# The front of a hybrid mixer step: the conditioning constants moved to the head of the load queue, the first products and the filter steps in a new order

## The chip, the cores and the metric

The kernel runs on one core of a Trainium2 chip. Its time is the device time of one execution in microseconds (us), as the median of three runs.

Engines are TensorE (PE in the profile, its weight loads PEld), VectorE (DVE), ScalarE (ACT), GpSimd (POOL) and SyncE (SP, which issues most loads). Each engine works through its own queue of instructions in order and waits on semaphores of the others.

## The reference

One layer of a hybrid mixer for 128 prompt tokens and 512 sample tokens, D = 1024. Everything begins with an adaptive modulation and one wide projection:

```python
def modulation(cond, w_ada, b_ada):
    mod = jax.nn.silu(cond) @ w_ada + b_ada
    return jnp.split(mod, 3, axis=-1)
...
    shift, scale, gate = modulation(cond, p["w_ada"], p["b_ada"])
    h = x * (1 + scale) + shift
    (v_h, x1, x0, g_h), (q, k, v, g_a), m = split_projection(h, p["w_in"], p["conv_w"], p["conv_b"])
```

There are two conditions, one for the prompt and one for the samples. From h one branch computes a gated long convolution (Hyena), whose filters come from a small network with two sine layers:

```python
    hf = jnp.sin(f_freq[0] * (z @ f_w1 + f_b1))
    hf = jnp.sin(f_freq[1] * (hf @ f_w2 + f_b2))
    hf = (hf @ f_w3).astype(jnp.float32).reshape(L, 2, D_HYENA)
```

The other branch is a neighbourhood attention. Both are gated, projected, merged, projected again, and a layer norm closes the step.

## The kernel before

**Numbers.** Products are made in three passes of a faster fp32 type: operands are split into a high and a low part (`hH`, `hL` of h, `wf`, `wg` of a weight in the front, `wh`, `wl` behind it), and hH·wf, hH·wg and hL·wf are summed. One such pass over one block of 128 rows is two matmuls, one for each half of the 640 tokens; one product of a row in the front is thus six matmuls.

**The front** is `prologue()`. It walks over the eight blocks k of 128 channels ("rows" here). For each row

- SP loads two tiles of `wada` (ada k and ada 8+k, 512 KB each, the shift and the scale), and one tile `xw` (the block of x, and of the weights of three output tiles 0, 8 and 1; 512 KB),
- TensorE multiplies the condition `st` with them (`adaT`, 16 matmuls, which the trace shows as 32 records since these run as full fp32 in two steps), ScalarE copies the result to `row` (L315), TensorE turns it to columns (`modT`, L342), and DVE adds the bias (`mod`, L347),
- ScalarE makes hH (L355), DVE makes hx (L354), wg (L357) and hL (L358),
- TensorE adds the row's products to three pairs of banks ("0k", "8k", "1k").

The script sets where the products stand: `script[k]` has four places, ahead of ada k, ahead of ada 8+k, ahead of modT and behind hL. In row k stand the products of row k-1, so that TensorE has work while mod is made. An item "w17" is 17 filler matmuls on zeros.

**The condition.** `st` is the silu of the condition, made of `pack0` (L297 to L300: tanh on ScalarE, two steps on DVE). pack0 (17 KB) is loaded by ScalarE's queue. All other loads here go through SP in the order of the program; a load also waits where its buffer is not free yet.

**The filter network** runs beside it as a generator of small steps (`sin_layer`, L225 to L246): matmuls `ps_f` and their release from PSUM by DVE, five to six steps of range reduction on DVE, and the sine on ScalarE. `layers[k]` says how many steps are taken in row k behind the row copy, and how many behind the products. Its input `zemb` is padded to 128 rows. The PSUM banks for adaT, modT and ps_f rotate over one pool of four buffers, of which the third pair of banks (`mm1lo`, `mm1hi`) holds two.

Behind the front, a list scheduler orders the Hyena stage by its own rules; its decisions depend on what came before. There ScalarE splits weights (`wl` L159, `wh` L161; GpSimd's accumulating load L160 completes wl), copies finished projections (`zs`), applies the short convolution (`x`, `u` L556, with `tap` L559 that GpSimd adds at L560), and splits filter tiles (`sh`, L111), which TensorE transforms in `fa` (L168).

Of the kernel before, what the change touches and what calls it, by code (L numbers as in the profile page):

```python
# [49 lines left out]
def tile_hyena_natten_step(ctx: ExitStack, tc: tile.TileContext, a, o):  # L50
# [14 lines left out]

    def load_to(dst, src, eng=None):
        ins = (eng or nc.sync).dma_start(dst, src)
        last[:] = [ins]
        if pinned[0]:
            tc.keep_in_program_order(ins)  # L70
# [50 lines left out]

    def load_pack(i, eng=None):
        pack = const.tile([P, sum(n for _, n in PACKS[i])], F32, tag=f"pack{i}", name=f"pack{i}")
        load_to(pack[:], a[f"pack{i}"], eng)
        c0 = 0
        for name, n in PACKS[i]:
            out[name] = pack[:, c0 : c0 + n]
            c0 += n

    v_d = dram.tile([4, P, 1280], F32, tag="v_d", name="v_d")  # L130

    load_pack(0, nc.scalar)
    cc, sel = out["cc"], out["sel"]
# [41 lines left out]
    def accumulate(ps, w, k, xh, xl, lead=(0, 1, 2)):  # L175
        passes = (w[0], xh), (w[0], xl), (w[1], xh)
        for i in lead:
            wt, x = passes[i]
            for hf in range(2):
                nc.tensor.matmul(  # L180
                    ps[hf][:, :HALF], wt[k], x[:, hf * HALF : (hf + 1) * HALF],
                    start=(i == 0 and k == 0), stop=(i == lead[2] and k == NK - 1), skip_group_check=True,
                )
# [41 lines left out]
    def sin_layer(fs, products, dst):  # L225
# [3 lines left out]
        for i, r0, w, x in products:  # L229
            at = {} if len(ps) == 1 else dict(tile_position=(64 * i, r0))  # L230
            nc.tensor.matmul(ps[i][r0 : r0 + w.shape[1], :320], w, x, start=True, stop=True, skip_group_check=True, **at)
        for i, p in enumerate(ps):
            nc.vector.tensor_scalar(ar[:, 320 * i : 320 * i + 320], p[:, :320], fs[:, 0:1], fs[:, 1:2], op0=ALU.add, op1=ALU.mult)
# [36 lines left out]
    def prologue():  # L270
        script = (
            ("w17", "", "w2", "w6"), ("", "", "00", "80 10"), ("", "", "01", "81 11"), ("", "", "02", "82 12"),
            ("", "", "03", "83 13"), ("", "", "04", "84 14"), ("", "", "05", "85 15"), ("", "", "06", "86 16 07 87 17"),
        )
        layers = ((0, 0), (0, 2), (0, 3), (0, 3), (1, 1), (0, 2), (0, 2), (0, 1))
        nc.vector.memset(f(hid[:, :256]), 0.0)
# [3 lines left out]
        def work(items):  # L280
            for item in items.split():
# [3 lines left out]
                else:  # L285
                    i, j = int(item[0]), int(item[1])
                    c = P * front.index(i)
                    accumulate(banks[i], [{j: t[:, c : c + P]} for t in parts[j]], j, hH[:, j], hL[:, j], lead=(0, 2, 1))

# [16 lines left out]
        for k in range(NK):  # L306
            xw = wp.tile([P, 1024], F32, tag="raw", bufs=3, name=f"xw{k}")
            psa = aux(f"adaT{k}")
            pool, tag = ((hw, "X"), (hyc, "dftL"), (hw, "F"))[k % 3]
            wt = pool.tile([P, 2048], F32, tag=tag, name=f"ada{k}")  # L310
            for part in range(2):
                work(script[k][part])
                ada(part * 8 + k, psa[:, part * P : part * P + P], wt[:, 1024 * part : 1024 * part + 1024])
            row_ = hwa.tile([P, 2 * P], F32, tag="fb", bufs=3, name=f"row{k}")
            nc.scalar.activation(row_[:], psa[:, : 2 * P], AF.Copy)  # L315
            load_to(xw[:], a["xw"][k])
            if k == 1:
                out["zemb"] = temp("u", "zemb", 4)[:, :448]
                load_to(out["zemb"], a["zemb"])
                load_pack(1)  # L320
# [18 lines left out]
            psm = aux(f"modT{k}")  # L339
            work(script[k][2])  # L340
            for c in range(2):
                nc.tensor.matmul(  # L342
                    psm[:, c * 2 : c * 2 + 2], row_[:, c * P : c * P + P], sel,
                    start=True, stop=True, skip_group_check=True,
                )
            mod = const.tile([P, 2, 2], F32, tag="mod", bufs=4, name=f"mod{k}")
            nc.vector.tensor_tensor(  # L347
# [4 lines left out]
            for c, s0, n in ((0, PC, LP), (1, SC, LS)):  # L352
                cs = slice(s0, s0 + n)
                nc.vector.tensor_scalar(hx[:, cs], xt[:, cs], mod[:, 1, c : c + 1], mod[:, 0, c : c + 1], op0=ALU.mult, op1=ALU.add)  # L354
                nc.scalar.activation(hH[:, k, cs], xt[:, cs], AF.Identity, scale=mod[:, 1, c : c + 1], bias=mod[:, 0, c : c + 1])  # L355
            if k < 6:
                nc.vector.tensor_tensor(wl, wf, f(wh), op=ALU.subtract)  # L357
# [7 lines left out]
            work(script[k][3])  # L365
            step(layers[k][1])
        now(filt)
# [1262 lines left out]
def _host_constants():  # L1630
    f32 = np.float32
    zs, decs = [], []
    for L in (LS, LP):
# [10 lines left out]
        else:  # L1644
            zs.append(z)
            decs.append(dec)
    zemb = np.zeros((128, 320))
    for i, z in enumerate(np.split(np.concatenate(zs, 0), 2)):
        zemb[64 * i : 64 * i + 33] = z.T
    decay = np.stack(decs).reshape(5, 128, 4, 256).transpose(1, 2, 0, 3)  # L1650
# [36 lines left out]
def _layout(inp):  # L1687
# [11 lines left out]
    b_ada = g["b_ada"][0]  # L1699
    fw1 = np.zeros((128, 128), np.float32)  # L1700
    for i in range(2):
        fw1[64 * i : 64 * i + 33, 64 * i : 64 * i + 64] = g["filt_w1"][0]
    w3 = g["filt_w3"][0].reshape(64, 2, 4, 256).transpose(0, 2, 1, 3).reshape(64, 4, 512)
# [70 lines left out]
```

## Time and profile before

| | us |
|---|---|
| median of 3 runs (860.24 to 860.34) | 860.33 |
| the profiled execution | 860.97 |
| its span | 859.1 |
| TensorE busy in the span | 846.8 |
| VectorE busy | 690.4 |
| ScalarE busy | 479.6 |
| GpSimd busy | 174.2 |

The span is the time from the first to the last instruction of the profiled execution; the rest of its 860.97 us lies around it. Busy time is an average over the whole; where TensorE stands idle and what ended that idle time is read from the waits and the timeline. "Releaser" is the instruction or transfer whose end let a waiting one start.

### The profile page before, as it was taken

The page shows a single profiled execution, that of the slowest core. Times are in us where ns is not written, and L with a number is a line of the kernel's source. Part 1 is how long each engine was busy: PE and PEld are TensorE (multiplying, and loading weights), DVE is VectorE, ACT ScalarE, POOL GpSimd, SP SyncE. Part 2 cuts the span into 40 slices and gives each one's busy share as a digit, 9 for nine tenths or more (in the row PEclk, how much of TensorE's full clock was granted, in tenths as well). Part 3 has the DMA queues.
Part 4 walks back from the last instruction along what each step waited for, and adds up shares of the span by engine and source line. Part 5 has one row for each costly group of instructions (what it writes and reads, how often), then busy time and mean ns, then how long its engine had stood idle before and what let it go on. Part 6 is the DMA issues. An engine that isn't in the chain of part 4 may idle for free.

```text
span 859.1 us, 16879 instructions
## 1 busy us (share of the span) xinstructions
PE 846.8 (99%) x6363; PEld 820.2 (95%) x6363; DVE 690.4 (80%) x1408; ACT 479.6 (56%) x1032; POOL 174.2 (20%) x172
## 2 busy tenths in 40 slices
PE   8999999999999999999999999999999999999996
PEld 7899999999999999999999999999999999999885
DVE  4786698697597688799797998989888678799776
ACT  4485666666656446566565565656656554345310
POOL 0010250242244010132222322224222200000000
PEclk9999999999999999999999999999999999999998
DMA  9896566566555677742636353454363386445621
GB/s 359 323 273 146 113 139 133 134 140 132 130 139 114 169 176 200 249 147 70 207 121 218 88 183 126 114 172 154 96 178 114 119 264 215 159 126 150 247 100 49
DMA packets 58120, 139.28 MB, mean 162 GB/s; under 512 B 8628, under 2 KB 25144, under 8 KB 58040
## 3 DMA queue, kind: packets, MB, share of 16 engines
q1 hardware_dynamic: 45944, 113.09, 39.7%
q0 software_dynamic: 5184, 18.09, 12.9%
q10 hardware_dynamic: 6912, 7.03, 2.4%
q8 instruction: 50, 0.82, 0.4%
q14 instruction: 30, 0.25, 0.1%
HBM read 120.76 MB, written 17.43 MB: 161 GB/s over the span
## 4 chain that ended last, share of the span: by engine, by line
PE 94%; DVE 2%; DMA 2%; POOL 1%; ACT 1%; issue 0%; DVEq 0%; SPq 0%
PE sp L1222 35%; PE mm L180 27%; PE out L1591 6%; PE v L950 5%; PE pt L1060 3%; PE s L1067 3%; PE s L1020 2%; DMA ada<-wada 2%; PE mm L194 2%; PE ve L962 1%; DVE wb L112 1%; POOL x L560 1%; PE yb L168 1%; PE yb L169 1%; PE yb L170 1%; PE ut L621 1%
## 5 line engine op out<-in xcount | busy, mean ns | idle before, releaser
L1222 PE MATMUL sp<-t,wb 128*128 128x320 f32 x1008 | 157.7, 310 | 0.1
L1222 PEld LDWEIGHTS sp<-t,wb 128*128 128x128 f32 x1008 | 149.1, 188 | 1.8 <-DVE wb L112 0.6
L1222 PE MATMUL sp<-hH,wb 128*128 128x320 f32 x504 | 121.6, 312 | 0.0
L111 ACT ACTIVATE wb<-s 128x512 fp32r<-128x512 f32 x100 | 61.1, 628 | 56.8 <-DVE s L1182 31.8
L180 PE MATMUL mm<-hL,wh 128*128 128x320 f32 x384 | 92.1, 309 | 0.0
L180 PE MATMUL mm<-hH,wh 128*128 128x320 f32 x384 | 91.5, 310 | 0.0
L180 PE MATMUL mm<-hH,wl 128*128 128x320 f32 x384 | 91.5, 309 | 0.0
L1222 PEld LDWEIGHTS sp<-hH,wb 128*128 128x128 f32 x504 | 86.5, 188 | 2.0 <-issue 1.8
L160 POOL DMA_DIRECT2D wl<-wall x33 | 28.7, 870 | 242.2 <-ACT wl L159 187.3
L1222 PE MATMUL sp<-hL,wb 128*128 128x320 f32 x252 | 77.7, 308 | 0.0
L112 DVE TENSOR_TENSOR wb<-s,wb 128x512 fp32r<-128x512 f32 x100 | 67.4, 686 | 4.4 <-ACT wb L111 4.3
L1042 POOL TENSOR_SCALAR p<-p,sm 128x384 f32<-128x384 f32 x32 | 46.9, 1476 | 108.8 <-DVE sm L1041 108.8
L111 ACT ACTIVATE wb<-raw 128x512 fp32r<-128x512 f32 x72 | 45.2, 628 | 42.5 <-PE sp L1222 30.6
L180 PEld LDWEIGHTS mm<-hL,wh 128*128 128x128 f32 x384 | 65.4, 188 | 0.6
L180 PEld LDWEIGHTS mm<-hH,wh 128*128 128x128 f32 x384 | 65.2, 188 | 0.6
L180 PEld LDWEIGHTS mm<-hH,wl 128*128 128x128 f32 x384 | 65.0, 188 | 0.1
L112 DVE TENSOR_TENSOR wb<-raw,wb 128x512 fp32r<-128x512 f32 x72 | 50.5, 702 | 5.0 <-ACT wb L111 5.0
L180 PE MATMUL mm<-yhs,wh 128*128 128x320 f32 x256 | 47.9, 309 | 0.0
L1222 PEld LDWEIGHTS sp<-hL,wb 128*128 128x128 f32 x252 | 47.3, 188 | 0.0
L161 ACT ACTIVATE wh<-raw 128x1024 fp32r<-128x1024 f32 x33 | 34.9, 1057 | 22.2 <-PE mm L180 14.0
L1237 DVE TENSOR_TENSOR c<-sp,u 128x320 f32<-128x320 f32 x75 | 36.2, 483 | 13.6 <-PE sp L1222 13.6
L1042 POOL TENSOR_SCALAR edge<-edge,sm 128x320 f32<-128x320 f32 x32 | 41.6, 1309 | 0.7 <-DVE sm L1041 0.5
(397 smaller groups left out, 2137.4 us busy)
## 6 DMA issues: line engine op xcount, KB each, us to landing
raw<-wall SPq DMA_DIRECT2D x93, 512.0 KB, 3.6
wl<-wall POOLq DMA_DIRECT2D x33, 512.0 KB, 5.8
ada<-wada SPq DMA_DIRECT2D x16, 512.0 KB, 9.5
tm<-bias SPq DMA_DIRECT2D x16, 512.0 KB, 4.7
xw<-xw SPq DMA_DIRECT2D x8, 512.0 KB, 8.4
gate<-wgate SPq DMA_DIRECT2D x8, 512.0 KB, 3.7
wo<-wall SPq DMA_DIRECT2D x8, 512.0 KB, 5.7
dec<-decay SPq DMA_DIRECT2D x20, 128.0 KB, 4.3
```

The costliest lines, as they stand in the source:

```text
L111: hi = nc.scalar.activation(dst_h, src, AF.Copy)
L112: return hi, (eng or nc.vector).tensor_tensor(dst_l, src, f(dst_h), op=ALU.subtract)
L160: nc.gpsimd.dma_start(wl, a["wall"][i], accum_op=ALU.add)
L161: nc.scalar.activation(wh, raw[:], AF.Copy)
L180: nc.tensor.matmul(ps[hf][:, :HALF], wt[k], x[:, hf * HALF : (hf + 1) * HALF], start=(i == 0 and k == 0), stop=(i == lead[2] and k == NK - ...
L950: nc.tensor.matmul(ps[t // 2][:, t % 2 * 256 : t % 2 * 256 + 256], x[:, k, P * t : P * t + P], wk, start=first and t % 2 == 0, stop=last, ...
L1042: nc.gpsimd.tensor_scalar_mul(pv, pv, sm[:, 2:3])
L1060: nc.tensor.transpose(pt[:, i * P : i * P + P], x, ident)
L1067: nc.tensor.matmul(dst, lhs, rhs, start=start, stop=stop, skip_group_check=True)
L1222: nc.tensor.matmul(dst, wk, x(xi, k), start=j < 4 and k == 0 and i == 0, stop=k == 3 and i == 2, skip_group_check=True,)
L1237: after = nc.vector.tensor_tensor(c, dst, c if j == 3 else u, op=ALU.add)
L1591: ins = nc.tensor.matmul(dst, m[k][:, c0 : c0 + P], w[:, c : c + n], start=(first and k == 0), stop=(last and k == 5), skip_group_check=True,)
```

## The change

1. pack0 is loaded by SP, first of all; the argument for another queue goes.
2. In row 0, 19 fillers instead of 17 stand ahead; one filler (before: two) now between the two modT matmuls; six behind as before. The row copy is made in two halves, each behind its half of adaT. DVE makes hH of the prompt columns, and wg ahead of hx.
3. Row 0's products are cut: "00a" are the passes with hH of product 0, "00b" the one with hL. In rows 1 and 2 they stand in other places, and row 2's two ada halves have product "01" between them.
4. `layers` has three numbers: the second counts steps behind modT. The first sine layer yields once more, behind its matmuls. In effect the first sine stands in row 4 instead of at the end of row 3, and the matmuls of the second layer behind modT of row 4.
5. zemb and its weights `fw1` are packed into 66 rows (2 x 33) instead of 128.

```diff
-    load_pack(0, nc.scalar)
+    load_pack(0)
...
+        yield
         for i, p in enumerate(ps):
             nc.vector.tensor_scalar(ar[:, 320 * i : 320 * i + 320], p[:, :320], fs[:, 0:1], fs[:, 1:2], op0=ALU.add, op1=ALU.mult)
         yield
...
         script = (
-            ("w17", "", "w2", "w6"), ("", "", "00", "80 10"), ("", "", "01", "81 11"), ("", "", "02", "82 12"),
+            ("w19", "", "w1", "w6"), ("00a", "", "80a", "10a 00b 80b 10b"), ("", "01", "81", "11"), ("", "", "02", "82 12"),
             ("", "", "03", "83 13"), ("", "", "04", "84 14"), ("", "", "05", "85 15"), ("", "", "06", "86 16 07 87 17"),
         )
-        layers = ((0, 0), (0, 2), (0, 3), (0, 3), (1, 1), (0, 2), (0, 2), (0, 1))
+        layers = ((0, 0, 0), (0, 0, 3), (0, 0, 3), (0, 0, 2), (1, 1, 2), (0, 0, 2), (0, 0, 2), (0, 0, 2))
+        passes = {"": (0, 2, 1), "a": (0, 2), "b": (1,)}
...
-                    accumulate(banks[i], [{j: t[:, c : c + P]} for t in parts[j]], j, hH[:, j], hL[:, j], lead=(0, 2, 1))
+                    accumulate(banks[i], [{j: t[:, c : c + P]} for t in parts[j]], j, hH[:, j], hL[:, j], lead=passes[item[2:]])
...
-            row_ = hwa.tile([P, 2 * P], F32, tag="fb", bufs=3, name=f"row{k}")
-            nc.scalar.activation(row_[:], psa[:, : 2 * P], AF.Copy)
+                if k == 0 or part:
+                    cs = slice(P * part if k == 0 else 0, P * part + P)
+                    nc.scalar.activation(row_[:, cs], psa[:, cs], AF.Copy)
...
-                out["zemb"] = temp("u", "zemb", 4)[:, :448]
+                out["zemb"] = temp("u", "zemb", 4)[:66, :448]
...
-            work(script[k][2])
+            if k:
+                work(script[k][2])
             for c in range(2):
+                if k == 0 and c:
+                    work(script[k][2])
...
+            step(layers[k][1])
...
-                nc.vector.tensor_scalar(hx[:, cs], xt[:, cs], mod[:, 1, c : c + 1], mod[:, 0, c : c + 1], op0=ALU.mult, op1=ALU.add)
-                nc.scalar.activation(hH[:, k, cs], xt[:, cs], AF.Identity, scale=mod[:, 1, c : c + 1], bias=mod[:, 0, c : c + 1])
-            if k < 6:
+                high = hH[:, k, cs], xt[:, cs]
+                scale, bias = mod[:, 1, c : c + 1], mod[:, 0, c : c + 1]
+                if k == 0 and c == 0:
+                    nc.vector.tensor_scalar(*high, scale, bias, op0=ALU.mult, op1=ALU.add)
+                    nc.vector.tensor_tensor(wl, wf, f(wh), op=ALU.subtract)
+                else:
+                    nc.scalar.activation(*high, AF.Identity, scale=scale, bias=bias)
+                nc.vector.tensor_scalar(hx[:, cs], xt[:, cs], scale, bias, op0=ALU.mult, op1=ALU.add)
+            if 0 < k < 6:
                 nc.vector.tensor_tensor(wl, wf, f(wh), op=ALU.subtract)
...
-            step(layers[k][1])
+            step(layers[k][2])
...
-    zemb = np.zeros((128, 320))
-    for i, z in enumerate(np.split(np.concatenate(zs, 0), 2)):
-        zemb[64 * i : 64 * i + 33] = z.T
+    zemb = np.concatenate([z.T for z in np.split(np.concatenate(zs, 0), 2)], axis=0)
...
-    fw1 = np.zeros((128, 128), np.float32)
+    fw1 = np.zeros((66, 128), np.float32)
     for i in range(2):
-        fw1[64 * i : 64 * i + 33, 64 * i : 64 * i + 64] = g["filt_w1"][0]
+        fw1[33 * i : 33 * i + 33, 64 * i : 64 * i + 64] = g["filt_w1"][0]
```

TensorE's queue from the start up to the second row's modT. "mm_0" and "mm_1" are the halves of product 0, hid holds the zeros of the fillers, and the number behind a name tells one buffer from another. Before:

```order
1 L284 MATMUL mm_0_131<-hid 128x256 x17
2 L265 MATMUL adaT_138<-ada_139,st 32x128 x16
3 L284 MATMUL mm_0_131<-hid 128x256 x2
4 L342 MATMUL modT_181<-pack_85,row_175 128x2 x2
5 L284 MATMUL mm_0_131<-hid 128x256 x6
6 L265 MATMUL adaT_202<-ada_203,st 32x128 x16
7 L180 MATMUL mm_0_131<-hH,wf_178 128x320
```

After:

```order
1 L286 MATMUL mm_0_131<-hid 128x256 x19
2 L266 MATMUL adaT_138<-ada_140,st 32x128 x16
3 L349 MATMUL modT_184<-pack_85,row_139 128x2
4 L286 MATMUL mm_0_131<-hid 128x256
5 L349 MATMUL modT_184<-pack_85,row_139 128x2
6 L286 MATMUL mm_0_131<-hid 128x256 x6
7 L180 MATMUL mm_0_131<-hH,wf_181 128x320
8 L180 MATMUL mm_1_132<-hH,wf_181 128x320
9 L180 MATMUL mm_0_131<-hH,wg_182 128x320
10 L180 MATMUL mm_1_132<-hH,wg_182 128x320
11 L266 MATMUL adaT_204<-ada_206,st 32x128 x16
```

Four products of row 0 have moved from behind the second adaT to ahead of it.

TensorE's queue in row 4, at the second sine layer's matmuls. hf is the first sine's result. Before:

```order
67 L265 MATMUL adaT_388<-ada_389,st 32x128 x16
68 L231 MATMUL ps_f_413<-hf_262,pack_227 128x320
69 L231 MATMUL ps_f_414<-hf_262,pack_227 128x320
70 L180 MATMUL mm_0_131<-hH,wf_351 128x320
```

After, from the last of product 0:

```order
75 L180 MATMUL mm_1_132<-hL,wf_353 128x320
76 L349 MATMUL modT_416<-pack_85,row_390 128x2 x2
77 L231 MATMUL ps_f_425<-hf_264,pack_233 128x320
78 L231 MATMUL ps_f_426<-hf_264,pack_233 128x320
```

The two matmuls have moved past six products and past modT.

ScalarE's queue where the Hyena stage begins (L556 is the short convolution, L570 in the new line numbers; L159 and L161 make the parts of the weight tile behind the next projection). Before:

```order
57 L553 ACTIVATE zs_107<-mm_1_132 128x8x40
58 L159 ACTIVATE wl_1036<-raw_1033 128x1024
59 L556 ACTIVATE u_669<-zs_107,pack_599 128x641
60 L382 ACTIVATE dftH<-draw 128x640 x2
61 L556 ACTIVATE u_723<-zs_115,pack_599 128x641
62 L161 ACTIVATE wh_1035<-raw_1033 128x1024
```

After:

```order
55 L567 ACTIVATE zs_107<-mm_1_132 128x8x40
56 L570 ACTIVATE u_671<-zs_107,pack_601 128x641
57 L396 ACTIVATE dftH<-draw 128x640 x2
58 L570 ACTIVATE u_725<-zs_115,pack_601 128x641
59 L159 ACTIVATE wl_1038<-raw_1035 128x1024
60 L161 ACTIVATE wh_1037<-raw_1035 128x1024
```

The first part of wl has moved behind four other activations. Further on the split `sh` of a filter tile has moved past three taps and part of a short convolution. Before:

```order
134 L556 ACTIVATE x_1_1473<-zs_107,pack_599 128x128
135 L559 ACTIVATE tap_17_0_1585<-zs_107,pack_599 128x128
136 L556 ACTIVATE x_1_1473<-zs_107,pack_599 128x512
137 L559 ACTIVATE tap_17_0_1588<-zs_107,pack_599 128x128
138 L559 ACTIVATE tap_17_129_1592<-zs_107,pack_599 128x512
139 L111 ACTIVATE sh_0_1152<-sd_1_1148 128x512
```

After:

```order
132 L570 ACTIVATE x_1_1475<-zs_107,pack_601 128x128
133 L111 ACTIVATE sh_0_1154<-sd_1_1150 128x512
134 L573 ACTIVATE tap_17_0_1587<-zs_107,pack_601 128x128
135 L570 ACTIVATE x_1_1475<-zs_107,pack_601 128x512
136 L573 ACTIVATE tap_17_0_1590<-zs_107,pack_601 128x128
```

Only one short convolution is left ahead of it.

## Rows read from the trace of the kernel before

**Rows 1.** Page, part 4: the chain that ended last, share by engine.

```profile
PE 94%; DVE 2%; DMA 2%; POOL 1%; ACT 1%; issue 0%; DVEq 0%; SPq 0%
```

**Rows 2.** Busy by stretch: length, busy time of each engine, clock, DMA share, GB/s.

```profile
0.00:45.00 45.00, 41.43 (x458) 36.51 (x459) 27.10 (x61) 21.46 (x40) 0.87 (x16) 1.00 0.90 340
...
20.00:25.00 5.00, 5.00 (x86) 4.55 (x78) 4.16 (x10) 2.00 (x4) 0.00 (x0) 1.00 1.03 415
```

**Rows 3.** TensorE's waits from 0 to 46 us: total, times, longest.

```profile
PE adaT L265 <- DMA ada<-wada: 0.9, 1, 0.9
PE ps_f L231 <- ACT hf L244: 0.7, 1, 0.7
PE adaT L265 <- DVE st L300: 0.5, 1, 0.5
```

**Rows 4.** Timeline, row 0: start, busy us, engine, line, instruction, [idle before <-releaser].

```profile
4.89 0.22 ACT L297 ACTIVATE th<-pack 128x16 f32<-128x16 f32 x1 [2.45 <-DMA pack<-pack]
...
5.66 1.69 PE L265 MATMUL adaT<-ada,st 128*32 128x128 f32 x32 [0.49 <-DVE st L300]
...
8.70 1.20 ACT L355 ACTIVATE hH<-xw,mod 128x128 fp32r<-128x128 f32 x2 [0.48 <-DVE mod L347]
```

**Rows 5.** DMA issues, 0 to 40 us: count, size, median us from issue to landing.

```profile
pack<-pack ACTq DMA_DIRECT2D x1, 17.0 KB, 4.1
```

**Rows 6.** Chain of the first 48 us, pieces in order: start, us, what.

```profile
0.73 0.39 SPq L67
...
6.03 9.92 DMA ada<-wada
```

**Rows 7.** Timeline of TensorE, row 2's second half, then all of row 3.

```profile
15.99 0.65 PE L265 MATMUL adaT<-ada,st 128*32 128x128 f32 x16 [0.95 <-DMA ada<-wada]
...
19.84 1.08 PE L265 MATMUL adaT<-ada,st 128*32 128x128 f32 x32
20.85 0.56 PE L180 MATMUL mm<-hH,wf 128*128 128x320 f32 x2
...
21.82 0.50 PE L342 MATMUL modT<-pack,row 128*128 128x2 f32 x4
22.19 0.54 PE L180 MATMUL mm<-hH,wf 128*128 128x320 f32 x2
...
24.13 1.08 PE L265 MATMUL adaT<-ada,st 128*32 128x128 f32 x32
```

**Rows 8.** Timeline of all engines around the second sine layer, row 4.

```profile
23.80 0.83 DVE L358 TENSOR_TENSOR hL<-hx,hH 128x640 fp32r<-128x640 f32 x1
...
25.80 0.37 ACT L315 ACTIVATE row<-adaT 128x256 f32<-128x256 f32 x1
25.94 1.07 PE L231 MATMUL ps_f<-hf,pack 64*128 64x320 f32 x4 [0.74 <-ACT hf L244]
...
26.79 1.13 DVE L233 TENSOR_SCALAR E<-ps_f,pack 128x320 f32<-128x320 f32 x2 [1.40 <-PE ps_f L231]
...
30.23 0.97 PE L265 MATMUL adaT<-ada,st 128*32 128x128 f32 x28
```

**Rows 9.** Timeline and landings around the weight tile wl10.

```profile
50.72 1.06 ACT L159 ACTIVATE wl<-raw 128x1024 fp32r<-128x1024 f32 x1 [0.26 <-DMA raw<-wall]
51.68 0.91 ACT L556 ACTIVATE u<-zs,pack 128x641 f32<-128x641 f32 x1
52.49 1.35 ACT L382 ACTIVATE dftH<-draw 128x640 fp32r<-128x640 f32 x2
...
52.11 1.00 POOL L160 DMA_DIRECT2D wl<-wall  x1 [50.70 <-ACT wl L159]
...
60.65 0.31 PE L180 MATMUL mm<-hH,wl 128*128 128x320 f32 x1
...
DMA to landing us min/median/max: 5.2/5.8/8.5
```

**Rows 10.** Timeline of TensorE where the front's Hyena filter is transformed.

```profile
118.08 0.39 PE L168 MATMUL fa<-sh,dftH 128*128 128x256 f32 x1 [0.63 <-ACT sh L111]
```

More of the change, by code (lines that the diff above doesn't have):

```diff
@@ L64, in tile_hyena_natten_step, with load_to @@
     last = []
-    def load_to(dst, src, eng=None):
-        ins = (eng or nc.sync).dma_start(dst, src)
+    def load_to(dst, src):
+        ins = nc.sync.dma_start(dst, src)
         last[:] = [ins]
@@ L120, in tile_hyena_natten_step, with load_pack @@
     yu_d, yh_d, ya_d, mh_d, ma_d = (dram.tile([NK, P, NT], F32, tag=t, name=t) for t in ("yu_d", "yh_d", "ya_d", "mh_d", "ma_d"))
-    def load_pack(i, eng=None):
+    def load_pack(i):
         pack = const.tile([P, sum(n for _, n in PACKS[i])], F32, tag=f"pack{i}", name=f"pack{i}")
-        load_to(pack[:], a[f"pack{i}"], eng)
+        load_to(pack[:], a[f"pack{i}"])
         c0 = 0
@@ L181, in accumulate @@
                     ps[hf][:, :HALF], wt[k], x[:, hf * HALF : (hf + 1) * HALF],
-                    start=(i == 0 and k == 0), stop=(i == lead[2] and k == NK - 1), skip_group_check=True,
+                    start=(i == 0 and k == 0), stop=(i == lead[-1] and k == NK - 1), skip_group_check=True,
                 )
@@ L308, in prologue @@
             psa = aux(f"adaT{k}")
+            row_ = hwa.tile([P, 2 * P], F32, tag="fb", bufs=3, name=f"row{k}")
             pool, tag = ((hw, "X"), (hyc, "dftL"), (hw, "F"))[k % 3]
```

## The prediction

> **What bounds the kernel now.** I read the chain of work that ended last first, then the busy times of the stretch that the change touches, then TensorE's waits in it, and last the timeline around each wait. The chain is 94% TensorE [rows 1], so time is won only where TensorE stands idle or does less. In the first 45 us, which hold all eight rows of the front, it is busy 41.43 us [rows 2]: 3.57 us are idle. Three waits in it have a name that the change touches: 0.5 us for the condition `st`, 0.9 us for a wada tile, 0.7 us for the filter network's first sine [rows 3]. They sum to 2.1 us. Behind the front one more wait matters: 0.63 us at 118.08 us, where `fa` waits for ScalarE's `sh` [rows 10].
>
> One more resource is full in the front: the load queue. At 20 to 25 us it moves 415 GB/s at a DMA share above 1 [rows 2]. A 512 KB tile then takes 524,288 B / 415 GB/s = 1.26 us, and a row's three tiles take 3.8 us. A row that waits for nothing takes TensorE 24.13 - 19.84 = 4.29 us [rows 7]. So TensorE is the slower of the two, but the stream starts behind it: only the first rows can be bound by data.
>
> All sums are made against the profiled execution, 860.97 us, of which 859.1 are the span. It lies 0.64 us above the median of 860.33 us; I take gains from the trace and subtract them from the median.
>
> **Part 1, the condition first.** `pack0` was issued on ScalarE's queue and took 4.1 us to land [rows 5]; the tanh waited for it until 4.89 us, and TensorE 0.49 us for `st` [rows 4]. At the head of SP's queue it should need no more than those 4.1 us, and with nothing beside it less: I take 2 to 2.5 us, an estimate from the 4.1 us that it took beside five 512 KB loads, with 4.1 as the other end. Then `st` is there well before the fillers end. The price is on SP: every load behind it is issued one issue later, 0.39 us by the chain's first piece [rows 6]. Against this, zemb shrinks from 128 to 66 rows of 1,792 B: 111 KB less, 0.27 us at 415 GB/s. So the stream behind row 1 moves by +0.39 - 0.27 = +0.12 us; bounds: -0.27 (pack0 costs the stream nothing) and +0.39 (the short zemb saves nothing).
>
> No row here has a tile of 66 partitions. A rule speaks against the saving: the Trainium skill, "DMA: Bandwidth & Descriptors", section "Why a DMA increments its semaphore by 16 and not by 1", says that such a transfer runs on the largest number of engines up to 16 that divides the row count, for 66 rows 11 engines. By it eleven engines carry six rows each instead of eight, and a later tile that needs all sixteen would gain only a quarter of zemb's old 0.55 us, 0.14 us. The stream would then move by +0.25 us, within the bounds above.
>
> **Part 2, rows 0 to 2.** Two more fillers stand in the 0.49 us of waiting, and adaT0 starts somewhere between 5.17, where the old fillers end, and the old 5.66 us [rows 4]; I take 5.4. A wait is added: the second half of adaT0 writes the bank from which ScalarE copies the first half, so it waits for that copy, at most the 0.37 us of a whole row copy [rows 8] plus the releases. Everything on TensorE is queued behind it. With the second copy, mod0 is no earlier than before, 0 to 0.3 us later. But the first products no longer need hL0, only hH0, of which ScalarE now makes one piece (before: 1.20 us for two, from 8.70 us, [rows 4]): ready at about 9.55 us.
>
> From there TensorE has work without a break. I take the spacings of an undisturbed row [rows 7]: adaT 1.01, six products 0.97, modT 0.37, twelve products 1.94 (0.16 each); the two zemb matmuls are half of four `ps_f` at 1.07 [rows 8], 0.5. Four products (9.55 to 10.2), adaT1 (11.2), four products (11.85), modT1 (12.2), ten products (13.8), zemb (14.3), first half of adaT2 (14.8), row 1's first six products (15.8). The second half of adaT2 needs the tile that came at 6.03 + 9.92 = 15.95 [rows 6]: with the stream's +0.12 it starts at 16.1 instead of 15.99. So the 0.95 us of waiting [rows 7] become about 0.3, and six products that lay behind that wait lie ahead of it. Then half an adaT (0.5), six products, modT2, six products: adaT3 can start at 18.9 instead of 19.84. Now data is late: two tiles follow the one of 15.95 before ada11, which lands at 15.95 + 3 x 1.26 = 19.73, plus 0.12. The second half of adaT3 starts at 19.9, and the row's products at 20.4 instead of 20.85. **Gain about 0.4 us**; at the bounds of the stream 0.15 and 0.85. If mod0 is 0.3 us late, this data wait swallows it.
>
> Row 3's tiles are 3.8 us further on and TensorE's next row 4.29 us: from row 4 the data is ahead.
>
> **Part 3, the filter steps.** In row 4 the four `ps_f` matmuls stood right behind adaT4 and waited 0.74 us for the sine `hf`, until 25.94 us [rows 8]. Now they stand behind six products and modT4, 0.97 + 0.37 us later on the queue: at about 26.1 us with the 0.4 us gained. The sine follows DVE's work of row 3 and one more row copy on ScalarE and should be there by 25.8. The wait goes: **0.74 us**. What is late next? DVE now takes `ps_f` out of its banks behind hL4, not ahead of mod4, and adaT5 needs one of these banks. hL3 ended at 24.63, 2.81 us behind the start of modT3 [rows 7, 8]. With modT4 at 25.6, hL4 ends at 28.4, the first half of the two additions (1.13 us, [rows 8]) at 29.0, the second at 29.5. adaT5 is ready at 30.23 - 1.14 = 29.1 [rows 8]. The first bank is in time, the second would cost 0.4 us: I take 0, since the banks come free in turn, and keep 0.4.
>
> The front thus ends about 1.14 us earlier (0.9 to 1.6).
>
> **Part 4, behind the front.** The edits also change the scheduler's order through the Hyena stage. Two places matter. At 118 us `sh` ran on ScalarE behind a tap that waits for GpSimd. In the new order sh stands ahead of all but one of the row's short-convolution steps and of all its taps. So the 0.63 us go [rows 10], unless another wait takes their place: **0.63 us**, the other end 0.
>
> The other place gets worse: wl10. ScalarE's part of it now stands behind two `u` activations and two `dftH` copies instead of ahead of them. By their spacing, 0.81 us for a u and 1.26 for the copies (about their 1.35 of busy time less the overlap, [rows 9]), it starts 2.88 us after 50.46 (where the old one still waited 0.26 us for data), at 53.34 on the old clock. GpSimd's accumulating load is issued 1.39 us behind (50.72 to 52.11), at 54.73, and lands 5.8 us later at the median: 60.53. TensorE needs it at 60.65 [rows 9]. The slack is 0.12 us instead of 2.7. The landings of these loads go from 5.2 over 5.8 to 8.5 us; nearest is the median, which costs nothing, but the slack is less than their scatter. I charge 0.2 us and keep 0 and 2.6.
>
> **The sum.** 0.4 + 0.74 + 0.63 - 0.2 = 1.57 us; 860.33 - 1.57 = **858.8 us**.
>
> **Rivals.**
> - *Data-bound*: the stream loses the whole 0.39 us, and the split's wait pushes row 0. Then rows 0 to 3 give 0.15 us instead of 0.4, the rest stays: 859.0. For: a DMA share above 1. Against: zemb is shorter.
> - *The waits move*: the sine's wait returns as adaT5's wait for its bank (0.4), and the fa wait is replaced by one of like size in the Hyena stage, where ScalarE, DVE and GpSimd release each other by turns: 0.4 + 0.74 - 0.4 - 0.2 = 0.54, so 859.8. For: a view of waits shows no slack, and the order of many rows changes. Against: before, only one such wait reached TensorE there.
> - *Slower*: wl10's load lands like the slowest of its kind, 8.5 us after issue [rows 9]. Then TensorE stands 2.6 us at about 59.5 us; with 1.14 us gained in the front and the fa wait unchanged the end is 860.33 + 1.44 = 861.8. It costs something from a landing above 5.9 us and makes the change slower from 7.1 us. Against: the median of the 33 loads is 5.8 us.
> - *It doesn't do what it says*: pack0 lands 4.1 us after issue at the head of SP's queue as well, `st` stays at 5.4 us, the split's wait comes on top, and only the filter wait is won: 859.6.
>
> **How the numbers follow.** Forecast 0.50 (858.3 to 859.2), waits that move 0.28, data-bound 0.12, slower 0.05, not as it says 0.05. The range goes from the upper ends of the front and of fa (1.6 + 0.63, less a little for wl10: 858.2) to the second rival with the low end of the front (0.9 - 0.4 - 0.2 = 0.3: 860.0). A measurement of this kernel tells about 0.2% from no change, 1.7 us. Faster than 858.6 is the better part of the forecast, 0.33; slower than 862.05 is the slow rival with a lost front besides, 0.03; the rest, 0.64, is within.
>
> **What would show it.** Right: the tanh near 3 us instead of 4.89 and no wait for `st`; the wait for ada at row 3's second half and a short one in row 2; no wait of `ps_f` for hf, and adaT5 1.1 us earlier than 30.23; no wait of fa at 117 us. Wrong: a wait of adaT5 for DVE, one of mm for wl at 59 to 60 us, or waits between 45 and 840 us that sum to more than 0.7 us. The forecast fails most easily in the Hyena stage, where slack is not visible.

## The result and the profile after

The changed kernel took 862.04 us (median of 16 runs, 861.69 to 862.59) where the kernel before took 860.34 in the same runs (859.80 to 860.69): +1.70 us, a ratio of 1.0020 with an interval of 1.0012 to 1.0027. The forecast was 858.8, in a range of 858.2 to 860.0.

In the front the waits went as the prediction said. TensorE's waits from 0 to 46 us and from 46 to 840 us in the changed kernel (total, times, longest), against [rows 3] and [rows 10]:

```profile
PE mm L286 <- DVE hid L278: 1.2, 1, 1.2
PE adaT L266 <- ACT row L319: 0.4, 1, 0.4
PE mm L180 <- DVE wg L366: 0.3, 1, 0.3
...
PE mm L180 <- DMA wl<-wall: 1.2, 1, 1.2
PE fb L169 <- DVE sl L112: 0.7, 1, 0.7
PE fb L168 <- ACT sh L111: 0.6, 1, 0.6
```

The three waits of the front that the change aimed at are gone, and so is the one of `fa`. In their place stand the predicted wait for the row copy (0.4) and one of 0.3 us for `wg`, and behind the front three new ones that sum to 2.5 us. The timeline of the changed kernel, against [rows 4] and [rows 8]:

```profile
2.62 0.21 ACT L299 ACTIVATE th<-pack 128x16 f32<-128x16 f32 x1 [0.62 <-DMA pack<-pack]
...
5.53 0.64 PE L266 MATMUL adaT<-ada,st 128*32 128x128 f32 x16
6.57 0.64 PE L266 MATMUL adaT<-ada,st 128*32 128x128 f32 x16 [0.40 <-ACT row L319]
...
25.78 1.13 PE L231 MATMUL ps_f<-hf,pack 64*128 64x320 f32 x4
...
28.79 1.08 PE L266 MATMUL adaT<-ada,st 128*32 128x128 f32 x32
```

The tanh runs at 2.62 instead of 4.89 us, `ps_f` waits for nothing, and adaT5 starts 1.44 us before the 30.23 of [rows 8].

That 1.44 us is too much, because the profiled execution of the kernel before was late. Two more profiles of the unchanged kernel (below) took 860.53 and 860.34 us, with adaT5 at 29.99 and 29.68 us. The one at 860.34, exactly the median, is the better base. Its busy times by stretch (length, busy time of PE first, ...), and then those of the changed kernel:

```profile
0.00:45.00 45.00, 41.52 (x462) 36.67 (x463) 27.65 (x63) 22.04 (x43) 0.87 (x16) 1.00 0.91 344
45.00:117.00 72.00, 71.89 (x498) 71.11 (x497) 51.85 (x78) 47.71 (x99) 16.11 (x14) 1.00 0.67 163
117.00:119.00 2.00, 1.47 (x9) 1.38 (x10) 1.49 (x2) 2.00 (x6) 1.30 (x1) 1.00 0.06 12
119.00:840.00 721.00, 720.90 (x5330) 701.13 (x5329) 596.03 (x1245) 407.59 (x886) 156.27 (x141) 1.00 0.54 154
```

```profile
0.00:45.00 45.00, 43.02 (x469) 37.80 (x470) 28.77 (x64) 22.87 (x46) 0.87 (x16) 1.00 0.92 348
45.00:117.00 72.00, 70.76 (x490) 69.91 (x490) 54.91 (x80) 46.89 (x95) 16.74 (x14) 1.00 0.64 160
117.00:119.00 2.00, 2.00 (x16) 2.00 (x15) 1.90 (x2) 1.38 (x2) 1.16 (x2) 1.00 0.03 8
119.00:840.00 721.00, 719.58 (x5321) 699.63 (x5320) 591.95 (x1240) 408.00 (x890) 154.88 (x142) 1.00 0.53 154
```

TensorE's idle time goes from 0.11 to 1.24 us in the second stretch, from 0.53 to 0 in the third, from 0.10 to 1.42 in the fourth: +1.92 us. The front gives 29.68 - 28.79 = 0.89 back. The balance is +1.03 us of the 1.4 by which the spans differ (858.5 and 859.9). (The profiled execution of the changed kernel, 861.69 us, is the fastest of its 16, so the spans show 1.4 of the 1.70 us between the medians.)

The last 0.4 us lie at the same waits. Matmuls of 0.31 us start 0.15 us apart, so their records overlap, and the idle time of a wait is counted only from the end of the last record. The changed kernel around the wait for wl:

```profile
59.35 0.31 PE L180 MATMUL mm<-hL,wh 128*128 128x320 f32 x1
60.91 0.56 PE L180 MATMUL mm<-hH,wl 128*128 128x320 f32 x2 [1.24 <-DMA wl<-wall]
61.31 0.45 PE L180 MATMUL mm<-hH,wh 128*128 128x320 f32 x2
```

Without the wait the pair behind it would have started at 59.50 us. It started 1.41 us later, and its first record was longer, so that the next pair followed 0.40 us behind and not 0.29: 1.52 us are lost, not 1.24. The waits at `fb` and the old one at `fa` cost 0.26 to 0.27 us beside their idle time in the same way (their first matmuls took 0.39 instead of 0.28 us). Three such waits came and one went, 0.54 us by this estimate. From adaT5 to the first `v` matmul at 273 us the changed kernel takes 2.37 us more (244.30 against 241.94), where idle time alone gives 2.56 - 0.63 = 1.93 and the estimate 2.47.

### The profile page after: what moved, and what is told of

Same layout as the page of the kernel before. It is cut to its first block, busy times and chain, and to the rows that moved or that the text cites. A ratio compares the mean times of both kernels' runs of the same rounds, so it can differ in the third digit from the quotient of the medians.

```text
span 859.9 us, 16885 instructions
## 1 busy us (share of the span) xinstructions
PE 847.3 (99%) x6364; PEld 820.0 (95%) x6364; DVE 691.5 (80%) x1409; ACT 479.7 (56%) x1032; POOL 173.7 (20%) x172
## 4 chain that ended last, share of the span: by engine, by line
PE 91%; DMA 3%; ACT 2%; DVE 2%; POOL 1%; issue 0%; SPq 0%; DVEq 0%
PE sp L1236 35%; PE mm L180 25%; PE out L1605 6%; PE v L964 5%; PE pt L1074 3%; PE s L1081 3%; PE s L1034 2%; DMA ada<-wada 2%; PE mm L194 2%; PE ve L976 1%; DMA wl<-wall 1%; POOL x L574 1%; DVE wb L112 1%; PE yb L169 1%; PE yb L168 1%; PE yb L170 1%
## 5 line engine op out<-in xcount | busy, mean ns | idle before, releaser
L161 ACT ACTIVATE wh<-raw 128x1024 fp32r<-128x1024 f32 x33 | 34.9, 1059 | 32.7 <-PE mm L180 24.5
```

The lines of the kernel that those rows point to most:

```text
L161: nc.scalar.activation(wh, raw[:], AF.Copy)
```

## The experiments

All were compared with the kernel before on the same chip. Ratios are to those runs.

| kernel | us, median (runs) | ratio, 95% interval |
|---|---|---|
| e1: the change, old filter steps | 860.37 (11) | 0.9998, 0.9990 to 1.0007 |
| e2: before, new filter steps alone | 862.60 (5) | 1.0033, 1.0020 to 1.0046 |
| e3: the change, old loads | 862.45 (6) | 1.0030, 1.0018 to 1.0041 |
| e4: before, new loads alone | 860.17 (11) | 0.9995, 0.9986 to 1.0004 |
| e5, e8: before, unchanged | 860.53, 860.34 (1 each) | |
| e6: the change, wl10 ahead | 859.46 (11) | 0.9990, 0.9981 to 0.9999 |
| e7: the change, one step moved | 860.00 (11) | 0.9995, 0.9986 to 1.0004 |
| e9: the change, wl3 without its load | 860.15 (11) | 0.9998, 0.9989 to 1.0006 |
| e10, e12: old rows, wl10 ahead | 859.17, 859.30 (11 each) | 0.9988, 0.9979 to 0.9997; 0.9987, 0.9978 to 0.9996 |
| e11: as e10, wh10 later | 858.80 (11) | 0.9978, 0.9970 to 0.9987 |

**Which part brings the loss?** The filter steps were undone alone, and done alone; the order of the scheduler's instructions told beforehand that the Hyena stage turns from the old order into the new one with this part, and with no other.

```diff
# e1, against the change
-        layers = ((0, 0, 0), (0, 0, 3), (0, 0, 3), (0, 0, 2), (1, 1, 2), (0, 0, 2), (0, 0, 2), (0, 0, 2))
+        layers = ((0, 0, 0), (0, 0, 2), (0, 0, 3), (0, 0, 3), (1, 0, 1), (0, 0, 2), (0, 0, 2), (0, 0, 1))
...
-        yield
         for i, p in enumerate(ps):
```

> The changed kernel with the filter network's steps where they stood before (the first sine at the end of row 3, the second layer's matmuls right behind adaT4, no extra yield). With it the Hyena stage has the order of the kernel before again, but for a few rows at its start. Theory A (the new order of the Hyena stage, which the filter steps bring about, costs more than the front wins): the front keeps the gain of rows 0 to 3, 0.8 us by the trace (row 3's products at 20.07 instead of 20.85), loses the 0.74 us of the sine's wait again, and has no wait for wl at 61 us nor for fb at 122 and 124 us: about 859.5 us, 0.8 below the kernel before. Theory B (the first products without low parts, the split row or the loads cost time that shows in the medians): the time stays above 861.

```diff
# e2, against the kernel before
-        layers = ((0, 0), (0, 2), (0, 3), (0, 3), (1, 1), (0, 2), (0, 2), (0, 1))
+        layers = ((0, 0, 0), (0, 0, 3), (0, 0, 3), (0, 0, 2), (1, 1, 2), (0, 0, 2), (0, 0, 2), (0, 0, 2))
...
+            step(layers[k][1])
             mod = const.tile([P, 2, 2], F32, tag="mod", bufs=4, name=f"mod{k}")
...
-            step(layers[k][1])
+            step(layers[k][2])
...
+        yield
         for i, p in enumerate(ps):
```

> The kernel before with the new filter steps alone. The Hyena stage then has the order of the changed kernel. Theory A: the front wins 0.74 us at ps_f and nothing else, the wl wait (1.2 us) and the two fb waits (1.3 us) appear and the fa wait (0.6 us) goes: 860.3 - 0.74 + 1.9 = about 861.5 us. Theory B: 859.6 us (only the filter wait goes).

e1 came back to 860.37 us and has neither the wl wait nor one for fb: the loss is the new order of the Hyena stage. But it did not reach 859.5, so the 0.8 us that I had read as the gain of rows 0 to 3 are not there. e2 has the three new waits in its trace (1.3, 0.7 and 0.6 us), and is 1.1 us slower than expected even so. About half of that is what two waits more cost beside their idle time (0.54 us, see above); the rest stays open. Its profiled execution shows something else, in the timeline and in the view by stretch:

```profile
5.32 0.22 ACT L298 ACTIVATE th<-pack 128x16 f32<-128x16 f32 x1 [2.88 <-DMA pack<-pack]
...
6.08 1.93 PE L266 MATMUL adaT<-ada,st 128*32 128x128 f32 x32 [0.92 <-DVE st L301]
...
10.95 1.94 PE L266 MATMUL adaT<-ada,st 128*32 128x128 f32 x32
...
17.14 1.08 PE L266 MATMUL adaT<-ada,st 128*32 128x128 f32 x32
```

```profile
6.00:8.00 2.00, 1.92 (x33) 1.42 (x33) 0.17 (x3) 1.04 (x2) 0.00 (x0) 1.00 1.03 420
```

In this execution (864.43 us, the upper end of e2's five; the lower three lie at 862.3 to 862.6) pack0, on ScalarE's queue, came at 5.3 us, TensorE waited 0.92 us, and then the 32 records of adaT took 1.93 and 1.94 us in rows 0 and 1, and 1.08 from row 2 on. The granted clock of 1.00 in the view by stretch says nothing for that time: the trace's first clock record, of the full clock (2.4 GHz), begins at 13.94 us, and the view counts time without a record as 1.00. Ahead of the first record matmuls are longer in every profile that has some on both sides of it: a filler takes 0.42 us ahead and 0.28 behind at the median, and a record of adaT in e2 and e3 0.42 and 0.27. That record begins at 4.7 to 7.4 us in twelve of the fourteen profiles, and at 13.94 and 14.08 us in those of e2 and e3 (864.77 us, the upper end of e3's six). There adaT5 starts at 31.17 and 31.53 us, against 28.62 to 28.93 in the other profiles with the new filter steps. So these two executions lost over 2 us to a slow start; why TensorE stayed slow for so long in them stays open.

**The loads.**

```diff
# e3, against the change (e4 is the reverse, against the kernel before)
-    load_pack(0)
+    load_pack(0, nc.scalar)
...
-                out["zemb"] = temp("u", "zemb", 4)[:66, :448]
+                out["zemb"] = temp("u", "zemb", 4)[:, :448]
```

> The changed kernel with pack0 on ScalarE's queue again and zemb padded to 128 rows again. Theory A: the Hyena order stays the changed one. st comes at 5.4 us, as before, so adaT0 starts near 5.7 and its second half, which waits for the first row copy, ends near 7.7 instead of 7.2; row 1 and 2 are 0.5 us later unless the second half of adaT2 or row 3 waits for data anyway: 0 to 0.5 us above the changed kernel, 862.0 to 862.5 us. Theory B: if pack0 at the head of the load queue is what costs, the time falls to about 861 or below.

> The kernel before with pack0 first on SP's queue and the short zemb alone. The Hyena order is that of before. Theory A: the 0.49 us for st go, but row 1's second half waited for its tile until 10.0 us anyway and row 2's until 15.95, so the sum moves only with the stream: 860.3 us, within 0.3 either way. Theory B: the stream is later by one issue and the time rises by 0.4 us or more.

e3 is at the upper end of what theory A expected, e4 within its bounds. In e4 adaT5 starts at 29.54 us, and row 2 waits for no tile (row 1 for one, 0.56 us). So the new loads do no harm, and are worth 0.14 to 0.45 us in the front against the two later profiles of the kernel before. By intervals the time of e4 cannot be told from no change.

**Was the base disturbed?** e5 and e8 are the unchanged kernel.

> The kernel before, unchanged, profiled once more. Its first profiled execution took 0.6 us more than its median. Theory A (the 0.95 us wait for ada10 in row 2 belonged to that one execution): the wait is shorter by some 0.5 to 0.7 us, adaT5 starts at 29.5 to 29.8 us instead of 30.23, and the span is near 858.4. Theory B (the wait belongs to the kernel): adaT5 at 30.2 us, and what rows 0 to 3 won was lost elsewhere.

> The kernel before, profiled a third time, as a second look beside the other one: the same expectations. If the two differ in row 0 or 2, what differs is the scatter that pack0's landing or one tile's landing brings.

The second half of adaT2 in e5, then in e8, against 15.99 in [rows 7]:

```profile
15.74 0.64 PE L265 MATMUL adaT<-ada,st 128*32 128x128 f32 x16 [1.10 <-DMA ada<-wada]
```

```profile
15.44 0.64 PE L265 MATMUL adaT<-ada,st 128*32 128x128 f32 x16 [0.80 <-DMA ada<-wada]
```

Neither theory is quite right: the wait belongs to the kernel (0.80 to 1.10 us in all three profiles), but the time at which it ends scatters by 0.55 us, and the profile that I worked from was the latest of the three.

**Rows 0 to 2.** e10 has the fillers, the row copy and the order of products of the kernel before, with all the rest new (and wl10 ahead, see e6).

```diff
# e10, against the kernel before: the new loads, the new filter steps, and
         next(head)
+        early[10] = wtile(10, "dma")
         dft_high(0, 1)
```

> The version with wl10 ahead of the dftH copies, but with the fillers and the order of the products of rows 0 to 2 as in the kernel before (the row copy in one piece, first products with all passes); new loads and new filter steps stay. Theory A (rows 0 to 2 gain nothing of their own, since the tiles of rows 1 to 3 arrive when they do): adaT5 starts within 0.2 us of 28.6 to 28.9 and the time is within 0.3 us of the version with the new rows, 859.46. Theory B (the new rows win the 0.4 us that the prediction gave them): 859.9 or more.

adaT5 in e1, e4, e6 and e10 (e1 and e6 with the new rows, e4 and e10 with the old ones; e1 and e4 with the old filter steps):

```profile
29.58 1.08 PE L265 MATMUL adaT<-ada,st 128*32 128x128 f32 x32
```

```profile
29.54 1.08 PE L265 MATMUL adaT<-ada,st 128*32 128x128 f32 x32
```

```profile
28.64 1.08 PE L266 MATMUL adaT<-ada,st 128*32 128x128 f32 x32
```

```profile
28.68 1.08 PE L266 MATMUL adaT<-ada,st 128*32 128x128 f32 x32
```

With either set of filter steps the rows' order moves adaT5 by 0.04 us: it wins nothing that shows, as profiles with the same rows scatter by 0.29 us there (28.64 to 28.93 in the changed kernel, e6, e7 and e9). The reason stands one row further on, in the second half of adaT3 in e6 (new rows), then in e12 (old rows):

```profile
19.34 0.64 PE L266 MATMUL adaT<-ada,st 128*32 128x128 f32 x16 [0.27 <-DMA ada<-wada]
```

```profile
19.34 0.64 PE L266 MATMUL adaT<-ada,st 128*32 128x128 f32 x16 [0.15 <-DMA ada<-wada]
```

Both orders wait for the same tile, ada11, and go on together. The filter steps move adaT5 by 0.86 to 0.94 us. In the times, old rows are even a little lower (859.17 and 859.30 against 859.46), which the intervals don't separate.

**The wait for wl10.** e6 makes its parts by hand ahead of the dftH copies; e7 leaves the order to the scheduler, with another distribution of the last filter steps.

```diff
# e6, against the change
         next(head)
+        early[10] = wtile(10, "dma")
         dft_high(0, 1)
# e7, against the change: the end of layers
-... (0, 0, 2), (0, 0, 2))
+... (0, 0, 3), (0, 0, 1))
```

> The changed kernel with the parts of weight tile wl10 made in the hand-set order ahead of the two dftH copies; the scheduler's order behind it shifts too, and sh of the third filter class stands one tap earlier. Theory A: GpSimd's load of wl10 is issued 1.3 us earlier, near 52.0, and the wait for wl (1.24 us) goes; with the earlier sh the first fb wait (0.58 us) goes too, the second (DVE beside GpSimd, 0.74) may stay: 862.0 - 1.8 = 860.2 us, 859.5 if all go. Rival (the wait is set by the load's landing among other loads, not by ScalarE's order): the wait stays at 1 us and the time above 861.

> The changed kernel with one filter step moved from row 7 to row 6 (three and one instead of two and two), nothing else by hand. The scheduler then gives the Hyena stage a third order: sh of the third class stands one tap earlier than in the changed kernel. Theory A (the loss is the scheduler's order, not the front): the time differs from the changed kernel's by what its waits differ, with the front unchanged (adaT5 at 28.8 us): 859.5 to 861. Theory B (the loss lies in the front's new order): 862.0 us unchanged.

Both are faster than the changed kernel by 2.0 to 2.6 us with the same rows 0 to 5 (adaT5 at 28.64 and 28.93 us). Neither has a wait for fb; the wl wait is 0.4 and 0.5 us. But the load of wl10, issued 1.4 us earlier in e6, still landed late, 7.7 us after issue and not 5.8. What slows it? The first guess was the next accumulating load, of wl3, which GpSimd issues 1.9 us behind it in the changed kernel and 4.75 behind before.

```diff
# e9, against the change
-        lo, hi = yield from proj(i, eng="dma")
+        lo, hi = yield from proj(i, eng="dma" if i != 3 else None)
```

> The changed kernel in which the low part of the next weight tile, wl3, is made by DVE from the loaded tile and not by GpSimd's accumulating load. wl10 keeps its late place behind two u and two dftH activations. Theory A1 (two accumulating loads, issued 53.32 and 55.19 in the changed kernel, slow each other: wl10 landed 7.5 us after issue instead of 5.8): wl10 lands 5.2 to 6 us after an issue near 53.3, before 59.3, and the wait for wl (1.24 us) is gone or under 0.2. Theory A2 (it is the late issue alone, and 7.5 us is what the load takes at that time): the wait stays at 1 us or more. The total follows, if the rest of the order stays alike: 860.5 to 861 by A1; DVE has 1.2 us more to do, and the scheduler's order behind it changes, so the wait itself decides, not the total.

e9's timeline, GpSimd's issue and TensorE, and then the landing of that one load:

```profile
53.20 1.00 POOL L160 DMA_DIRECT2D wl<-wall  x1 [51.80 <-DVE dftL L402]
...
60.68 0.56 PE L180 MATMUL mm<-hH,wl 128*128 128x320 f32 x2 [1.13 <-DMA wl<-wall]
```

```profile
DMA to landing us min/median/max: 7.4/7.4/7.4
```

That guess falls: without the other accumulating load it takes 7.4 us all the same. (e9 as a whole is 1.9 us below the changed kernel even so: its order has no wait at fb, see below.) The next suspect is a load of SP. Before, and in the changed kernel, SP's next 512 KB raw tile is issued at

```profile
55.63 0.33 SPq L67 DMA_DIRECT2D raw<-wall  x1
```

```profile
53.96 0.33 SPq L67 DMA_DIRECT2D raw<-wall  x1
```

that is 3.5 us behind wl10's load before (52.11, [rows 9]), and 0.64 us behind it in the changed kernel (53.32). It waits for the raw tile's buffer, which wh10 frees, and in the new order wh10 runs right behind wl10. e11 moves wh10 alone:

```diff
# e11, against e10 (wtile calls between() ahead of wh's activation)
-        early[10] = wtile(10, "dma")
-        dft_high(0, 1)
+        early[10] = wtile(10, "dma", between=lambda: dft_high(0, 1))
```

> The version with the old rows and wl10 ahead, in which only wh10, the last reader of the raw tile of wl10, moves behind the two dftH copies, 1.3 us later. The raw tile's buffer is what SP's next load of 512 KB waits for. Theory A3 (that load, issued 0.6 us behind wl10's accumulating load, takes the DMA engines from it; before it came 3.5 us behind): the raw load is issued near 53.9 instead of 52.6, wl10 lands 6 to 6.5 us after its issue instead of 7.6, and the wait for wl (0.4 us) is gone: 858.8 us. Rival A2 (the accumulating load is slow there for another reason): the landing stays at 7.5 and the wait at 0.4: 859.2.

> The version with the old rows and wl10 ahead once more, unchanged, beside the one with wh10 later on the same chip: 859.2 us, wl10 landing 7.6 us after issue, a wait for wl of 0.4 us. Both theories expect the same.

The timelines of e11 and of e12, each with the landing of wl10's load behind it: wl10's issue, the raw tile's issue, and in e12 TensorE's wait.

```profile
52.08 1.00 POOL L160 DMA_DIRECT2D wl<-wall  x1 [50.68 <-ACT wl L159]
...
53.98 0.33 SPq L67 DMA_DIRECT2D raw<-wall  x1
```

```profile
DMA to landing us min/median/max: 5.7/5.7/5.7
```

```profile
51.89 1.00 POOL L160 DMA_DIRECT2D wl<-wall  x1 [50.49 <-ACT wl L159]
...
52.53 0.33 SPq L67 DMA_DIRECT2D raw<-wall  x1
...
59.53 0.42 PE L180 MATMUL mm<-hH,wl 128*128 128x320 f32 x1 [0.34 <-DMA wl<-wall]
```

```profile
DMA to landing us min/median/max: 7.6/7.6/7.6
```

Issued 1.9 us ahead of the raw tile instead of 0.64, wl10 lands in 5.7 us instead of 7.6; e11 has no wait for wl, and 858.80 us against 859.30 on the same chip. The price of e12's wait of 0.34 us also shows in the traces: from adaT5 to the first `v` matmul e11 takes 240.99 us and e12 241.62, 0.62 us more. All fourteen profiles fall into line: where the raw tile's issue follows wl10's by 0.6 us (eight), wl10 lands after 7.4 to 7.7 us; where by 3.5 us (five), after 5.6 to 5.9. What was moved is wh10; that it acts through the raw load and not by itself is read from these times. e11 is the fastest version of the study, ahead of both kernels. The Trainium skill, "DMA: Bandwidth & Descriptors", section "Issuing engines are not separate DMA queues", says that transfers started by different engines end up on the same 16 DMA engines and interleave; these traces agree, with 1.9 us as the price here.

**The waits at fb** were not tried alone. e9 comes nearest: it keeps the wait for wl (1.13 us), loses both waits at fb, and takes 860.15 us against 862.04. In the changed kernel GpSimd, ScalarE, TensorE and DVE show this chain:

```profile
110.78 4.81 POOL L574 TENSOR_TENSOR x<-x,tap 128x128 f32<-128x128 f32 x1
...
115.62 0.40 ACT L573 ACTIVATE tap<-zs,pack 128x128 f32<-128x128 f32 x1 [4.23 <-POOL x L574]
...
117.62 0.72 ACT L573 ACTIVATE tap<-zs,pack 128x512 f32<-128x512 f32 x1 [1.59 <-POOL x L574]
...
121.49 0.64 ACT L111 ACTIVATE sh<-sd 128x512 fp32r<-128x512 f32 x1
122.16 1.97 DVE L112 TENSOR_TENSOR sl<-sd,sh 128x512 fp32r<-128x512 f32 x1 [3.23 <-ACT sh L111]
122.18 0.39 PE L168 MATMUL fb<-sh,dftH 128*128 128x256 f32 x1 [0.58 <-ACT sh L111]
...
124.19 0.39 PE L169 MATMUL fb<-sl,dftH 128*128 128x256 f32 x1 [0.74 <-DVE sl L112]
```

GpSimd's addition took 4.81 us, beside three large DVE instructions; ScalarE's taps wait for it one by one, and the sh that fb needs, the last in that queue, runs at 121.49. The DVE step behind it then took 1.97 us beside GpSimd's next addition, where the same step takes 0.68 with GpSimd at rest. But sh is not later than it was: in the kernel before it ran at 121.99 us, and TensorE came to fb only behind it:

```profile
123.75 0.28 PE L168 MATMUL fb<-sh,dftH 128*128 128x256 f32 x1
```

The changed order lets TensorE come to fb at 121.60, two microseconds earlier, and leaves sh about where it was. In e6, e7, e9 and e10 sh stands ahead of the last tap, and there is no wait. e10's rows:

```profile
113.38 0.62 ACT L111 ACTIVATE sh<-sd 128x512 fp32r<-128x512 f32 x1
...
116.95 0.72 ACT L561 ACTIVATE tap<-zs,pack 128x512 f32<-128x512 f32 x1 [2.96 <-POOL x L562]
```

Since other rows moved with it in all four, this cause rests on the chain and on these orders, not on an experiment of its own.

## Why the prediction was wrong, by its steps

- **Part 1, the condition: right for `st`, wrong for the stream.** pack0 landed 1.9 us after issue (2 to 2.5 taken), the tanh ran at 2.62, and st kept nobody waiting. The rule on 66 rows that the prediction cites can be tried on the trace: zemb's semaphore got sixteen updates at its landing in the kernel before (11.32 to 11.84 us), and in the changed one a single one right behind the issue (4.64 us) and eleven at the landing (11.58 to 11.92), which fits eleven engines and not sixteen. The stream behind it was not 0.12 us late: row 2's second tile landed at 14.60 us in the changed kernel, against 15.39 to 15.95 in the three profiles of the kernel before. It came at 14.34 to 15.11 in all with the new loads, but at 14.75 and 14.47 in e2 and e3 with the old ones as well, so what brings it forward is not shown.
- **Part 2, rows 0 to 2: wrong.** The term was 0.4 us, and measured it is nil (0.04 us at adaT5 in two pairs). The step that failed is the base: I took the tile's landing at 15.95 us as a fixed time, and it was the late end of a scatter of 0.55 us. With the new loads alone row 2 no longer waits for a tile at all, so the reordering has nothing to hide there, and in row 3 the tile of 19.3 us holds the new and the old order alike. The added wait for the row copy came as predicted (0.4 us).
- **Part 3, the filter steps: right.** 0.74 was the term, 0.86 to 0.94 measured at adaT5, more than the idle time as with the other waits; no TensorE wait for DVE took its place.
- **Part 4, fa: right.** Its 0.63 us are gone, and 0.27 with them.
- **Part 4, wl10: the mechanism was right, the size was wrong.** I had the late place and a slack of 0.12 us, and charged 0.2 us; it cost 1.24 us of idle time and 1.52 in all. The landing of 5.8 us came from a row in which the next large load followed 3.5 us behind. The order that I showed for the change has wh10 right behind wl10, which frees the buffer of the next raw load; I followed wl10's own chain and not what its neighbour releases. The rival "slower" priced just this mechanism with 8.5 us and held it unlikely; 7.5 was the answer. That its 861.8 lies so near the measured 862.04 is luck: it had the wait of fa still there, and none at fb.
- **Part 4, fb: missed.** I had looked at the one wait that the trace of before showed in the Hyena stage and asked whether it would go, and put "a wait of like size elsewhere" at 0.63 us. Two came, 1.32 us together and 1.85 with what they cost beside their idle time, for which the sum had no term at all.

The forecast thus had the front's sign and size (1.14 predicted, 0.89 measured against the base at the median), but its 0.89 came almost wholly from the filter steps. It lost on two places behind the front: 1.24 + 1.32 - 0.53 in idle time and about 0.5 more beside it, where it had counted on -0.43.

## What to carry to other kernels

When an edit in a front lets a list scheduler order later stages anew, price those stages first: undoing each part alone and comparing the orders shows which part turns them, before anything is timed. Where a load's slack becomes a tenth of a microsecond, look at which transfers its neighbours in the queue release, because two 512 KB loads issued 0.6 us apart do not land as one alone does. A wait of TensorE is dearer than its idle time says, here by about 0.27 us each. And before a wait of one profile becomes a term of a sum, see in a second profile whether it ends at the same time.

## What the runs showed of the hardware

- The same accumulating load of 512 KB took 5.7 us when SP's 512 KB load came 1.9 us behind it, and 7.6 us when it came 0.64 us behind.
- A load of 17 KB landed 1.9 us after issue at the head of SP's queue, and 4.1 us on ScalarE's queue beside the large loads; the tanh behind it ran at 4.67 to 5.32 us in five profiles with that arrangement, and at 2.41 to 2.95 us in nine with the new one.
- A wait in a row of matmuls costs more than TensorE's idle time: 1.52 us for a wait of 1.24, and 0.62 us between e11 and e12 for one of 0.34.
- Matmul records ahead of the trace's first clock record are longer (a filler 0.42 instead of 0.28 us); it began at 4.7 to 7.4 us in twelve profiles and at 13.9 to 14.1 us in two.
- GpSimd's addition of 128 x 128 elements took 2.85 us in the kernel before and 4.81 us in the changed one, according to what DVE did beside it; others of its size took 0.46 us (at 101.99 us in the changed kernel, beside DVE instructions with one input from PSUM). The Trainium skill, "GPSIMD Engine Reference", in its table of properties, says that GpSimd shares its SBUF interfaces with VectorE and contends with DVE instructions of two SBUF inputs; these rows agree, with 0.46 to 4.81 us for GpSimd, and a factor of 2.9 for DVE's own step. DVE's step took 0.67 us at 111.85 us, in a row of DVE instructions that had begun ahead of the addition of 4.81 us (109.05 against 110.78), and 1.97 us at 122.16, just behind the start of another addition (121.97).
